# A hybrid convolution and RWKV7 layer on one core: the rows of x transposed by products with a diagonal instead of normalised first

## The chip, the core and the metric

The kernel runs on one core of a Trainium2 chip. The metric is the device time of one execution in microseconds (us), the median over several runs. The engines of the core are TensorE (PE in the profile, its weight loads apart as PEld), VectorE (DVE), ScalarE (ACT), GpSimd (POOL) and SyncE (SP). SP does nothing here but issue DMAs; the queues of DMA issues are called SPq, ACTq and POOLq. Each engine takes its instructions in the order of the program, and an instruction that waits holds up all that stand behind it on its engine.

## The reference

One layer of a decoder over a prompt of 2048 positions and a sample of 8 sequences of 8 positions, D = 1024 columns. Cut to what matters:

```python
xn = rms_norm(x, norm_g)                 # x * rsqrt(mean(x*x) + 1e-6) * norm_g
p = xn @ w_in                            # 1024 -> 4 * 512 + 4 * 512 + 128 columns
# conv branch: u = C * h; causal convolution of width 3; out = B * z * silu(G)
# rwkv7 branch: two-tap token shift of its columns, decay and learning rate by small matrices,
#   S_t = S_{t-1} diag(w_t) + (S_{t-1} (-kk_t)) (kk_t * a_t)^T + v_t k_t^T ;  o_t = S_t r_t
#   per-head group norm, bonus, silu gate
y = concat(y_conv, y_rwkv) @ w_out
y_out = rms_norm(x + y, final_norm_g)
new_shift = xn[:, -1]                    # last normalised row of the prompt and of each sample sequence
```

All inputs and outputs are float32. The change concerns the first line alone, and `new_shift`, which are rows of its result.

## The kernel before, in words

The products with `w_in` contract over D, so they need the normalised rows with D on the partitions: xn transposed. The prompt is worked in two halves of 1024 positions; in each half the columns (positions) are split into three blocks, of 330 (74 for the sample, 256 prompt), 384 and 384 columns in the first half, of 256, 384 and 384 in the second. `xprep(hf)` (lines 211 to 290) prepares a half, block by block:

- Rows come in by SP's queue as tiles of 128 rows x 1024 columns (the sample as 64 x 1024), into staging tiles: four slots "hp", and once each "la" (la1), "wr" and "na", which belong to later stages (line 247).
- ScalarE squares each tile and adds up its rows (line 251); VectorE makes the inverse roots r of up to three tiles at once by three Newton steps on 128x3 (`rsqrt`, line 188).
- Each tile is multiplied by r (one number per row) and by the norm weight, which a DMA has spread over all 128 partitions in a tile "la" (`grow`): one VectorE instruction (line 267), or for the third tile of blocks 1 and 2 a ScalarE copy and a GpSimd product (lines 264 and 265).
- TensorE transposes the tile in pieces of 128x128, four to a PSUM bank "ax" (two buffers; lines 279 and 286).
- `split` (line 205) evacuates a bank: ScalarE rounds it to the high part "xh" (fp32r), VectorE subtracts that from the bank and gets the low part "xl".

`project` (line 309) makes 128 columns of p for each block with 24 matmuls into one PSUM bank "pj" (two buffers): xh by wh, xl by wh, xh by wl, for each of eight k.

The main loop (lines 930 to 972) goes through eight "pairs" of heads, four for each half. A pair projects its columns, forms chunk matrices, inverts triangular chunk matrices (`inverse`, line 640) and runs the recurrence (`wkv`). `inverse` begins with a chain of small VectorE steps on tiles "xi", "sub" and "na" (a forward substitution), whose result goes to DRAM in two DMAs as "dx" (line 669) and comes back re-ordered in twelve DMAs to tiles AB0, AB1, AB2 (line 678); VectorE then transposes each of these in blocks of 32 (line 680) for the next matmuls. `xprep(0)` stands at the start of the program; `xprep(1)` stands in pair 3, behind the last conv group of the first half and ahead of that pair's `inverse`. So the rows of the second half are prepared while the substitution of pair 3 runs on VectorE.

The program is written in that order, but the order of the instructions on each engine is laid out before the kernel runs, by a scheduler that takes the instructions of several generators as their inputs come due. It decides in which row of an engine's list a multiplication, a substitution step and an AB transposition stand.

The line numbers 117, 120, 123 and 129 are those of the helpers `copy`, `stt`, `tt` and `mm`, through which most instructions go; there the tiles tell them apart.

## Time and profile before

| | before |
|---|---|
| median of 3 runs | 1622.39 us (1618.18 to 1624.21) |
| the profiled execution | 1613.0 us, span of its instructions 1610.9 us |
| TensorE matmuls (PE) | 1512.1 us busy, 94% of the span, 11088 instructions |
| weight loads (PEld) | 1265.4 us, 79% |
| VectorE (DVE) | 1011.3 us, 63% |
| ScalarE (ACT) | 616.2 us, 38% |
| GpSimd (POOL) | 289.6 us, 18% |
| mean granted clock of TensorE | 0.969 |

The page of the profile cuts the span into 40 slices of some 40 us and prints the busy share of each engine in tenths:

```profile
PE   4999999999999999989999999999999999899997
DVE  6377458765687458784586358545864578466544
ACT  6443346324542354344541354135313543342221
```

TensorE is at 9 nearly everywhere, but at 4 in the first slice, which holds `xprep(0)`. A slice is too wide for `xprep(1)`, which falls into the eighteenth (685 to 725 us); it shows in windows of 10 us. The percentages are means over stages: what an edit is worth is read in the stage where it stands.

### The profile page before, as it was taken

How to read it: one execution, taken by the hardware profiler on the slowest of the kernel's cores; microseconds unless marked ns; L12 is line 12 of the kernel's file. 1: busy time of each engine (PE TensorE's matmuls, PEld its weight loads, DVE VectorE, ACT ScalarE, POOL GpSimd, SP SyncE). 2: the span in 40 equal slices, each digit the busy share in tenths (PEclk: the TensorE clock that was granted, in tenths of full speed). 3: DMA queues.
4: the chain of work that ended last, by engine and by line, in shares of the span. 5: the costliest groups of instructions: out<-in, count | busy, mean ns of one | idle time of the engine just before them, and what ended most of it. 6: DMA issues, size and time to landing. Idle time of an engine off the chain costs nothing.

```text
span 1610.9 us, 29335 instructions
## 1 busy us (share of the span) xinstructions
PE 1512.1 (94%) x11088; PEld 1265.4 (79%) x11088; DVE 1011.3 (63%) x3101; ACT 616.2 (38%) x1591; POOL 289.6 (18%) x395
## 2 busy tenths in 40 slices
PE   4999999999999999989999999999999999899997
PEld 4989778887788777877789678877897788567885
DVE  6377458765687458784586358545864578466544
ACT  6443346324542354344541354135313543342221
POOL 3134103311133112320022002200220022000000
PEclk9989999899999998999999899999999999899999
DMA  7323412342043213441124112411241145414441
GB/s 241 118 83 110 137 49 74 108 122 78 20 136 113 95 50 112 140 125 61 36 73 125 42 36 66 135 39 37 77 127 38 34 118 155 133 62 137 143 137 53
DMA packets 121967, 151.90 MB, mean 94 GB/s; under 512 B 62617, under 2 KB 86681, under 8 KB 121826
## 3 DMA queue, kind: packets, MB, share of 16 engines
q1 hardware_dynamic: 107024, 104.53, 21.2%
q0 software_dynamic: 9536, 34.64, 6.8%
q10 hardware_dynamic: 5266, 10.86, 1.9%
q8 instruction: 88, 1.44, 0.4%
q14 instruction: 53, 0.43, 0.1%
HBM read 92.60 MB, written 57.35 MB: 93 GB/s over the span
## 4 chain that ended last, share of the span: by engine, by line
PE 63%; DVE 23%; issue 5%; DMA 5%; ACT 2%; POOL 1%; SPq 1%; ACTq 0%; DVEq 0%; POOLq 0%
PE pj L129 41%; PE ca L129 5%; PE ax L129 5%; DVE sub L123 5%; PE cb L129 4%; DVE xi L123 4%; DVE hp L123 2%; PE oo L129 2%; PE cx L129 2%; DVE hp L120 1%; PE cx L703 1%; DVE bk L123 1%; DVE t L120 1%; DMA dx<-xi 1%; DMA AB<-dx 1%
## 5 line engine op out<-in xcount | busy, mean ns | idle before, releaser
L129 PE MATMUL pj<-xh,wh 128*128 128x384 f32 (+3 forms) x1856 | 655.4, 354 | 18.0 <-DVE hp L123 13.8
L129 PE MATMUL pj<-xl,wh 128*128 128x384 f32 (+3 forms) x1856 | 652.8, 352 | 2.7 <-POOL xl L207 2.1
L129 PE MATMUL pj<-xh,wl 128*128 128x384 f32 (+3 forms) x1856 | 650.9, 351 | 0.8 <-DMA wl<-wsp 0.8
L129 PEld LDWEIGHTS pj<-xh,wh 128*128 128x128 f32 x1856 | 356.7, 192 | 50.1 <-DVE hp L123 11.5
L129 PEld LDWEIGHTS pj<-xl,wh 128*128 128x128 f32 x1856 | 356.8, 192 | 31.7 <-POOL xl L207 3.0
L129 PEld LDWEIGHTS pj<-xh,wl 128*128 128x128 f32 x1856 | 355.8, 192 | 27.3 <-issue 1.7
L117 ACT ACTIVATE tS<-sv,wc 64x64 f32<-64x64 f32 x256 | 88.0, 344 | 114.8 <-DVE sv L120 94.2
L207 POOL TENSOR_TENSOR wl<-wr,wh 128x512 fp32r<-128x512 f32 x66 | 87.8, 1342 | 193.4 <-ACT wh L117 190.0
L120 DVE SCALAR_TENSOR_TENSOR sv<-cb,wc,tS 64x64 f32<-64x64 f32 x240 | 68.0, 283 | 62.6 <-PE cb L129 56.1
L129 PE MATMUL ax<-L,bk 64*128 64x128 f32 x528 | 79.1, 298 | 20.9 <-DVE bk L123 11.2
L129 PEld LDWEIGHTS ax<-L,bk 64*128 64x128 f32 x528 | 66.1, 197 | 37.9 <-issue 23.6
L123 DVE TENSOR_TENSOR sub<-xi,na 128x126 f32<-128x126 f32 (+22 forms) x248 | 81.5, 329 | 16.5 <-DMA na<-dn 9.7
L117 ACT ACTIVATE t<-pj,prm 128x384 f32<-128x384 f32 (+3 forms) x170 | 68.8, 433 | 54.5 <-PE pj L129 53.4
L751 DVE TENSOR_SCALAR u<-ca,Q 128x64 f32<-128x64 f32 x128 | 36.2, 283 | 82.3 <-PE ca L129 82.1
L531 POOL TENSOR_TENSOR bk<-t,t 64x384 f32<-64x384 f32 (+2 forms) x56 | 58.3, 1041 | 155.3 <-ACT t L503 72.9
L123 DVE TENSOR_TENSOR xi<-xi,sub 128x126 f32<-128x126 f32 (+22 forms) x248 | 77.6, 313 | 7.1
L117 ACT ACTIVATE wh<-wr 128x512 fp32r<-128x512 f32 x66 | 40.5, 626 | 92.0 <-PE pj L129 73.1
L129 PEld LDWEIGHTS ca<-sv,L 128*64 128x64 f32 x528 | 43.3, 134 | 37.2 <-DVE sv L120 12.8
L129 PE MATMUL ca<-sv,L 128*64 128x64 f32 x528 | 67.8, 245 | 0.1
L741 DVE COPY xs<-ca 128x64 f32<-128x64 f32 x128 | 28.7, 224 | 60.4 <-PE ca L129 50.6
L298 POOL DMA_DIRECT2D wh<-wsp x33 | 18.6, 565 | 254.1 <-PE pj L129 216.7
L123 DVE TENSOR_TENSOR hp<-pj,hp 128x512 f32<-128x512 f32 (+1 forms) x34 | 23.4, 689 | 62.6 <-PE pj L129 62.2
(207 smaller groups left out, 2057.4 us busy)
## 6 DMA issues: line engine op xcount, KB each, us to landing
wr<-in_w_in SPq DMA_DIRECT2D x66, 256.0 KB, 3.7
wsp<-wh SPq DMA_DIRECT2D x33, 512.0 KB, 3.1
wsp<-wl SPq DMA_DIRECT2D x33, 512.0 KB, 3.5
wh<-wsp POOLq DMA_DIRECT2D x33, 512.0 KB, 3.6
wl<-wsp POOLq DMA_DIRECT2D x33, 512.0 KB, 4.8
hp<-in_x_prompt SPq DMA_DIRECT2D x28, 512.0 KB, 4.1
la<-yd SPq DMA_DIRECT2D x16, 512.0 KB, 4.0
out_y_p<-hp ACTq DMA_DIRECT2D x16, 512.0 KB, 2.6
```

The source lines that it names most:

```text
L117: act.activation(out=out, in_=in_, func=AF.Copy, scale=scale, bias=bias)
L120: eng.scalar_tensor_tensor(out=out, in0=in0, scalar=scalar, in1=in1, op0=op0, op1=op1)
L123: dve.tensor_tensor(out=out, in0=in0, in1=in1, op=op)
L129: pe.matmul(out, lhsT=lhsT, rhs=rhs, start=start, stop=stop)
L207: eng.tensor_tensor(out=lo, in0=src, in1=hi.bitcast(F32), op=ALU.subtract)
L298: pool.dma_start(out=wh, in_=wsp[col, 0])
L531: pool.tensor_tensor(out=S.bk[bl.i][hs, chs, h, :], in0=ta[hs, a:a + n].rearrange("p (c j) -> p c j", j=64), in1=wi[hs, a:a + n].rearrange ...
L703: pe.transpose(out=pb[:, i, :], in_=S.bk[bi][:, ca + i].rearrange("p a t -> p (a t)"), identity=ident)
L741: dve.tensor_copy(out=xs_, in_=px)
L751: dve.tensor_scalar(out=u, in0=pu, scalar1=S.Q[:, q:q + 1], scalar2=None, op0=ALU.mult)
```

## The change

The rows are no longer normalised before they are transposed. For each tile of rows VectorE writes a diagonal matrix of the inverse roots (`dg`: the identity, each row times its r; line 260 of the changed kernel), and TensorE multiplies a raw piece of 128x128 by it, which transposes the piece and scales its rows at once. The pieces are ordered by k: one PSUM bank holds one k of all tiles of the block (256 or 384 columns), in turn in "ax", "ax", "cx" (and "oo" in the first half). The norm weight, which is one number per partition once D lies on the partitions, is applied at the evacuation: ScalarE copies the bank times `norm_g` to xh, VectorE forms bank times `norm_g` minus xh in one instruction. For that `norm_g` comes as eight further columns of the parameters; it is no longer spread over partitions for the row tiles. The sample's piece is first multiplied by the weight into a tile "c2" and then split. Since no normalised row exists any more, `shift_rows` computes the nine rows of `new_shift` apart, after the first pair's projections: nine rows loaded, squared, scaled and multiplied by a norm weight spread over nine partitions.

```diff
@@ -37,8 +37,8 @@
-P_MU, P_KK, P_KA, P_RK, P_LG, P_LB, P_W0, P_A0, P_CW = 0, 17, 21, 25, 29, 33, 37, 41, 45
-NPRM = 57
+P_MU, P_KK, P_KA, P_RK, P_LG, P_LB, P_W0, P_A0, P_CW, P_NG = 0, 17, 21, 25, 29, 33, 37, 41, 45, 57
+NPRM = 65
@@ -209,9 +209,6 @@
     WR = T("w", [128, KT, 128], "wr", 1)
 
     def xprep(hf):
-        grow = rowtile()
-        if hf == 1:
-            act.dma_start(out=grow, in_=I["norm_g"].partition_broadcast(128).rearrange("p a d -> p (a d)"))
         if hf == 0:
             act.dma_start(out=cst[:, 0:128], in_=I["consts"][:, 0:128])
         xh, xl = [], []
@@ -252,19 +249,18 @@
                                accum_out=ss[:n, j:j + 1])
                 xts.append(xt)
             if bl.samp:
-                sync.dma_start(out=grow, in_=I["norm_g"].partition_broadcast(128).rearrange("p a d -> p (a d)"))
                 sr = T("small", [128, 144], "sub", 1)[:, :KT * NB].rearrange("p (k b) -> p k b", k=KT)
                 act.dma_start(out=sr, in_=I["state_shift"])
                 load_params()
             dve.tensor_scalar(out=ss, in0=ss, scalar1=1.0 / D, scalar2=RMS_EPS, op0=ALU.mult, op1=ALU.add)
             r = rsqrt(ss, len(rows), 128, "n")
-            for j, xt in enumerate(xts):
-                n = rows[j][1]
-                if bl.i and j == 2:
-                    copy(xt, xt, scale=r[:n, j:j + 1])
-                    pool.tensor_tensor(out=xt, in0=xt, in1=grow[:n], op=ALU.mult)
-                else:
-                    stt(xt, xt, r[:n, j:j + 1], grow[:n])
+            dg = tmp()
+            offs, o = [], 0
+            for j, (_, n, _) in enumerate(rows):
+                dve.tensor_scalar(out=dg[:n, o:o + n], in0=ident[:n, :n], scalar1=r[:n, j:j + 1], scalar2=None,
+                                  op0=ALU.mult)
+                offs.append((o, n))
+                o += n
             if bl.samp:
                 pool.memset(h[:, :, 72:74].bitcast(F32), 0.0)
                 pool.memset(l[:, :, 72:74].bitcast(F32), 0.0)
@@ -272,22 +268,41 @@
                 lv = l[:, :, 0:72].rearrange("p k (b j) -> p k b j", j=9)
                 split(hv[:, :, :, 0], lv[:, :, :, 0], sr)
                 xt = xts.pop(0)
-                rows.pop(0)
-                pool.dma_start(out=O["shift_s"], in_=xt[7:SAMP:8, :])
+                offs.pop(0)
                 ps = AX([128, KT, SAMP])
                 for k in range(KT):
-                    pe.transpose(out=ps[:, k, :], in_=xt[:, k * 128:(k + 1) * 128], identity=ident[:SAMP, :SAMP])
-                split(hv[:, :, :, 1:9], lv[:, :, :, 1:9], ps.rearrange("p k (b j) -> p k b j", j=8))
-            for xt, (_, _, o) in zip(xts, rows):
-                for q in range(2):
-                    ps = AX([128, 4, 128])
-                    for k in range(4):
-                        kk = q * 4 + k
-                        pe.transpose(out=ps[:, k, :], in_=xt[:, kk * 128:(kk + 1) * 128], identity=ident)
-                    split(h[:, q * 4:q * 4 + 4, o:o + 128], l[:, q * 4:q * 4 + 4, o:o + 128], ps)
-            if hf == 1 and bl.i == 2:
-                act.dma_start(out=O["shift_p"], in_=xts[-1][127:128, :])
+                    mm(ps[:, k, :], xt[:, k * 128:(k + 1) * 128], dg[:SAMP, 0:SAMP])
+                sx = T("ch", [128, KT, SAMP], "c2", 4)
+                tt(sx, ps, prm[:, P_NG:P_NG + KT].unsqueeze(2).to_broadcast([128, KT, SAMP]), ALU.mult)
+                split(hv[:, :, :, 1:9], lv[:, :, :, 1:9], sx.rearrange("p k (b j) -> p k b j", j=8))
+            for k in range(KT):
+                tag, nb = (("ax", 2), ("ax", 2), ("cx", 1), ("oo", 1))[k % (4 if hf == 0 else 3)]
+                ps = PS([128, bl.np], tag, nb)
+                for i, (xt, (o, n)) in enumerate(zip(xts, offs)):
+                    mm(ps[:, i * 128:(i + 1) * 128], xt[:, k * 128:(k + 1) * 128], dg[:, o:o + n])
+                hk = h[:, k, bl.c0:bl.c0 + bl.np]
+                copy(hk, ps, scale=pcol(P_NG, k))
+                stt(l[:, k, bl.c0:bl.c0 + bl.np], ps, pcol(P_NG, k), hk.bitcast(F32), ALU.mult, ALU.subtract)
         return xh, xl
+    def shift_rows():
+        n = NB + 1
+        xt = T("pair", [128, 32, 32], "na", 1).rearrange("p a b -> p (a b)")[:n]
+        sync.dma_start(out=xt[0:NB], in_=I["x_sample"][7:SAMP:8, :])
+        sync.dma_start(out=xt[NB:n], in_=I["x_prompt"][SEQ - 1:SEQ, :])
+        junk = T("ch", [128, D], "c2", 4, BF16)[:n]
+        s = T("small", [128, 1], "ss", 2)[:n]
+        act.activation(out=junk, in_=xt, func=AF.Square, accum_out=s)
+        dve.tensor_scalar(out=s, in0=s, scalar1=1.0 / D, scalar2=RMS_EPS, op0=ALU.mult, op1=ALU.add)
+        r = rsqrt(s, 1, n)
+        for q in range(2):
+            m = slice(q * 512, (q + 1) * 512)
+            g = T("ch", [128, 512], "c2", 4)[:n]
+            sync.dma_start(out=g, in_=I["norm_g"].partition_broadcast(n).rearrange("p a d -> p (a d)")[:, m])
+            stt(xt[:, m], xt[:, m], r, g)
+        act.dma_start(out=O["shift_s"], in_=xt[0:NB])
+        act.dma_start(out=O["shift_p"], in_=xt[NB:n])
 
@@ -956,6 +971,8 @@
         if s == 3:
             run(conv_group(xs, hf, p))
             xs = xprep(1)
+        if s == 0:
+            shift_rows()
         run(inverse(S))
         wkv(S)
@@ -989,7 +1006,7 @@
-                                                    "conv_w")], axis=1),
+                                                    "conv_w", "norm_g")], axis=1),
```

Apart from the two stretches of `xprep` and the instructions of `shift_rows`, the lists of before and after hold the same instructions in the same order on each engine. Three places are shown. The numbers in a name tell tiles of one kind apart; a tile keeps its name through its life.

VectorE at the start, from the last step of the first inverse roots ("nwyn" is r; hp_22, hp_23 and hp_24 are the three row tiles of block 0, la0 the spread weight), before:

```order
L120 SCALAR_TENSOR_TENSOR nwyn_26_137<-nwan_27_138,nwyn_26_137 128x3
L120 SCALAR_TENSOR_TENSOR hp_22_121<-hp_22_121,nwyn_26_137,la0_18_115 64x1024
L120 SCALAR_TENSOR_TENSOR hp_23_124<-hp_23_124,nwyn_26_137,la0_18_115 128x1024
L120 SCALAR_TENSOR_TENSOR hp_24_127<-hp_24_127,nwyn_26_137,la0_18_115 128x1024
L207 TENSOR_TENSOR xl0_20_118<-ax_28_158,xh0_19_117 128x8x8x8
L259 TENSOR_SCALAR ssx_35_199<-ssx_35_199 128x3
L194 TENSOR_SCALAR nwan_40_211<-ssx_35_199 128x3
```

And after ("t" is the diagonal, "c2" the sample's weighted piece, cst holds the identity, prm the weight):

```order
L120 SCALAR_TENSOR_TENSOR nwyn_25_135<-nwan_26_136,nwyn_25_135 128x3
L260 TENSOR_SCALAR t_27_148<-cst_1_90,nwyn_25_135 64x64
L260 TENSOR_SCALAR t_27_148<-cst_1_90,nwyn_25_135 128x128 x2
L123 TENSOR_TENSOR c2_29_165<-ax_28_156,prm_4_95 128x512
L255 TENSOR_SCALAR ssx_40_211<-ssx_40_211 128x3
L194 TENSOR_SCALAR nwan_45_223<-ssx_40_211 128x3
L196 TENSOR_SCALAR nwyn_44_222<-nwan_45_223 128x3
L123 TENSOR_TENSOR nwan_45_223<-nwyn_44_222 128x3
L120 SCALAR_TENSOR_TENSOR nwan_45_223<-nwan_45_223,ssx_40_211 128x3
L120 SCALAR_TENSOR_TENSOR nwyn_44_222<-nwan_45_223,nwyn_44_222 128x3
L207 TENSOR_TENSOR xl0_19_117<-c2_29_165,xh0_18_116 128x8x8x8
L120 SCALAR_TENSOR_TENSOR xl0_19_117<-ax_30_169,prm_4_95,xh0_18_116 128x256
```

The three multiplications of whole tiles are gone, two kinds of diagonals stand in their place, and the roots of block 1 (ssx, nwan, nwyn) have moved up ahead of the sample's low part.

VectorE in the middle, where the second half is prepared; xl0, xl1 and xl2 are the low parts of its three blocks, and "na" out of AB0 is the block transposition in `inverse`. Before:

```order
L120 SCALAR_TENSOR_TENSOR hp_1224_7518<-hp_1224_7518,nwyn_1230_7531,la0_1191_7384 128x1024
L120 SCALAR_TENSOR_TENSOR hp_1226_7522<-hp_1226_7522,nwyn_1230_7531,la0_1191_7384 128x1024
L680 STREAM_TRANSPOSE na_1283_7725<-AB0_1065_6328 128x128
L207 TENSOR_TENSOR xl2_1222_7516<-ax_1232_7548,xh2_1221_7515 128x4x128
L207 TENSOR_TENSOR xl2_1222_7516<-ax_1233_7555,xh2_1221_7515 128x4x128
L680 STREAM_TRANSPOSE na_1283_7725<-AB1_1066_6329 128x192
L207 TENSOR_TENSOR xl2_1222_7516<-ax_1234_7562,xh2_1221_7515 128x4x128
L207 TENSOR_TENSOR xl2_1222_7516<-ax_1235_7569,xh2_1221_7515 128x4x128
```

And after:

```order
L120 SCALAR_TENSOR_TENSOR xl0_1210_7437<-ax_1219_7464,prm_4_95,xh0_1209_7436 128x256
L120 SCALAR_TENSOR_TENSOR xl0_1210_7437<-ax_1220_7469,prm_4_95,xh0_1209_7436 128x256
L120 SCALAR_TENSOR_TENSOR xl0_1210_7437<-cx_1221_7474,prm_4_95,xh0_1209_7436 128x256
L260 TENSOR_SCALAR t_1237_7532<-cst_1_90,nwyn_1235_7519 128x128
L120 SCALAR_TENSOR_TENSOR xl0_1210_7437<-ax_1222_7479,prm_4_95,xh0_1209_7436 128x256
L695 STREAM_TRANSPOSE na_1311_7799<-AB0_1083_6380 128x128
L120 SCALAR_TENSOR_TENSOR xl0_1210_7437<-ax_1223_7484,prm_4_95,xh0_1209_7436 128x256
L120 SCALAR_TENSOR_TENSOR xl0_1210_7437<-cx_1224_7489,prm_4_95,xh0_1209_7436 128x256
L120 SCALAR_TENSOR_TENSOR xl0_1210_7437<-ax_1225_7494,prm_4_95,xh0_1209_7436 128x256
L120 SCALAR_TENSOR_TENSOR xl0_1210_7437<-ax_1226_7499,prm_4_95,xh0_1209_7436 128x256
L695 STREAM_TRANSPOSE na_1311_7799<-AB1_1084_6381 128x192
L120 SCALAR_TENSOR_TENSOR xl1_1228_7505<-ax_1238_7536,prm_4_95,xh1_1227_7504 128x384
```

Before, the first transposition of AB0 stood behind the last multiplications of block 2; now it stands between the fourth and the fifth low part of block 0, and that of AB1 ahead of the first low part of block 1.

SP's queue in the middle; "dx" is the way out of the substitution, AB0 to AB2 the way back, "hp" from in_x_prompt the row loads, here those of block 2. Before:

```order
L247 DMA hp_1224_7518<-in_x_prompt 128x1024
L384 DMA yd02_86<-hp_1159_6982 128x384
L247 DMA hp_1226_7522<-in_x_prompt 128x1024
L247 DMA hp_1228_7526<-in_x_prompt 128x1024
L669 DMA dx_1282_7722<-xi_1239_7592 1024x1x32 x2
L678 DMA AB0_1065_6328<-dx_1282_7722 32x4x32 x4
L678 DMA AB1_1066_6329<-dx_1282_7722 32x6x32 x4
L678 DMA AB2_1067_6330<-dx_1282_7722 32x6x32 x4
```

And after:

```order
L684 DMA dx_1310_7796<-xi_1267_7666 1024x1x32 x2
L693 DMA AB0_1083_6380<-dx_1310_7796 32x4x32 x3
L399 DMA yd02_86<-hp_1177_7034 128x384
L693 DMA AB0_1083_6380<-dx_1310_7796 32x4x32
L693 DMA AB1_1084_6381<-dx_1310_7796 32x6x32 x3
L244 DMA hp_1249_7587<-in_x_prompt 128x1024
L244 DMA hp_1251_7591<-in_x_prompt 128x1024
L244 DMA hp_1253_7595<-in_x_prompt 128x1024
L693 DMA AB1_1084_6381<-dx_1310_7796 32x6x32
L693 DMA AB2_1085_6382<-dx_1310_7796 32x6x32 x4
```

The three row loads of block 2, which stood ahead of the dx transfers, now stand ahead of the fourth transfer of AB1.

## Rows read from the trace of the kernel before

**Rows 1.** Busy us by stretch (instruction counts in brackets), clock, DMA, columns in the first line

```profile
core 0: us, PE busy (x) PEld busy (x) DVE busy (x) ACT busy (x) POOL busy (x), PEclk, DMA share, GB/s
690.00:700.00 10.00, 5.58 (x34) 5.31 (x35) 9.31 (x31) 1.86 (x5) 2.42 (x5) 0.94 0.79 260
700.00:710.00 10.00, 10.00 (x64) 9.41 (x64) 5.71 (x14) 6.87 (x13) 0.78 (x3) 0.72 0.66 189
740.00:760.00 20.00, 20.00 (x185) 14.45 (x183) 9.62 (x35) 7.70 (x23) 1.05 (x2) 1.00 0.20 66
```

**Rows 2.** Chain of waits from the start: start us, us, engine, tile, line, instructions

```profile
44.38 38.96 PE pj L129 x233
```

**Rows 3.** Instructions on tile pj alone by stretch; columns PE, PEld, DVE, ACT, clock, DMA

```profile
0.00:44.38 44.38, 13.32 (x56) 10.70 (x57) 0.66 (x2) 1.31 (x4) 1.00 0.65 219
694.90:722.20 27.30, 15.77 (x81) 12.38 (x79) 1.50 (x3) 2.45 (x7) 0.87 0.48 136
```

**Rows 4.** Timeline, start: start us, us, engine line op out<-in, count [idle before <-releaser]

```profile
9.26 0.17 DVE L259 TENSOR_SCALAR ssx<-ssx 128x3 f32<-128x3 f32 x1 [0.31 <-ACT xl L251]
...
11.63 3.90 DVE L120 SCALAR_TENSOR_TENSOR hp<-hp,nwyn,la 64x1024 f32<-64x1024 f32 x3
...
12.96 1.11 PE L279 MATMUL ax<-cst,hp 64*128 64x64 f32 x8 [12.96 <-DVE hp L120]
...
16.19 2.11 PE L286 MATMUL ax<-cst,hp 128*128 128x128 f32 x8 [0.68 <-DVE xl L207]
```

**Rows 5.** Timeline of the middle, where the second half's rows are prepared

```profile
686.83 2.39 POOL L265 TENSOR_TENSOR wr<-wr,la 128x1024 f32<-128x1024 f32 x1 [14.64 <-ACT wr L117]
686.84 3.46 DVE L120 SCALAR_TENSOR_TENSOR hp<-hp,nwyn,la 128x1024 f32<-128x1024 f32 x1
...
690.82 0.45 PE L129 MATMUL pj<-xh,wh 128*128 128x384 f32 x1 [1.45 <-DVE t L120]
...
695.09 1.04 PE L286 MATMUL ax<-cst,hp 128*128 128x128 f32 x8
...
699.73 2.18 PE L286 MATMUL ax<-cst,hp 128*128 128x128 f32 x8 [3.60 <-DVE xl L207]
...
703.01 1.29 SPq L669 DMA_DIRECT2D dx<-xi  x2
...
708.92 6.66 SPq L678 DMA_DIRECT2D AB<-dx  x12
```

**Rows 6.** Nearest operations: timeline rows, and groups by form (busy us, mean ns | idle before)

```profile
651.14 0.90 PE L129 MATMUL ax<-L,bk 64*128 64x128 f32 x6 [0.87 <-DVE bk L123]
...
712.28 0.47 DVE L120 SCALAR_TENSOR_TENSOR t<-pj,omm,t 128x256 f32<-128x256 f32 x1
...
736.55 0.62 DVE L120 SCALAR_TENSOR_TENSOR t<-pj,omm,t 128x384 f32<-128x384 f32 x1 [0.86 <-ACT t L117]
...
L129 PE MATMUL ax<-L,bk 64*128 64x128 f32 x528 | 79.1, 298 | 20.9 <-DVE bk L123 11.2 <-DVE nwag L120 4.3 <-DVE L L123 3.0
...
L207 DVE TENSOR_TENSOR xl<-ax,xh 128x512 fp32r<-128x512 f32 x33 | 22.2, 687 | 9.0 <-ACT xh L117 8.9
...
L117 ACT ACTIVATE xh<-ax 128x512 fp32r<-128x512 f32 x33 | 19.2, 595 | 17.5 <-PE ax L286 14.9 <-POOL sv L775 2.1
...
L251 ACT ACTIVATE xl<-hp 128x1024 fp32r<-128x1024 f32 x6 | 6.3, 1054 | 3.3 <-DMA hp<-in_x_prompt 3.1
```

**Rows 7.** Timeline of pair 0, from the dx issues to the first AB transposition

```profile
167.32 1.30 SPq L669 DMA_DIRECT2D dx<-xi  x2
...
171.71 3.68 SPq L678 DMA_DIRECT2D AB<-dx  x8
...
174.52 0.30 DVE L680 STREAM_TRANSPOSE na<-AB 128x128 f32<-128x128 f32 x1
```

**Rows 8.** DMAs landed in 700 to 720 us: KB each, median us from issue to landing

```profile
hp<-in_x_prompt SPq DMA_DIRECT2D x2, 512.0 KB, 4.2
AB<-dx SPq DMA_DIRECT2D x8, 24.0 KB, 1.9
```

## The prediction

> **What bounds the kernel now.** I read the engines' busy time by stretch first, then the chain of waits for the start, then the timeline of the two stretches in which the rows of x are prepared. TensorE is the bound: it is busy for the whole of a normal stretch, 20.00 of 20 us at 740 [rows 1], and from 44.38 us on the chain runs for 38.96 us through 233 projection matmuls without a break, 0.167 us each [rows 2]. The rows are prepared twice, and only there is TensorE short of work: before 44.38 us, and from 690 to 722 us, where it sits idle and its granted clock falls to a mean of 0.72 from 700 to 710 [rows 1]. So the change is worth what it does to the moment at which the projections run unbroken, in each of the two places. What it saves on VectorE elsewhere costs nobody anything.
>
> In those two places the work of TensorE before "unbroken" is known: 56 projection matmuls had started by 44.38, and 81 by 722.2, three of them of the conv group before [rows 3]. I count against these.
>
> The profiled execution took 1613.0 us with a span of 1610.9; the median of the runs is 1622.39. I work in the profiled execution and add the difference to the median.
>
> **The change part by part.** *Removed:* 17 multiplications of a whole row tile. The 13 on VectorE cost 1.3 us each (three in 3.90) [rows 4], but 3.46 when GpSimd multiplied at the same time, as at 686.84 [rows 5]; the other four were a ScalarE copy and a GpSimd product. Also removed: 32 pairs of 512-wide evacuations, 0.59 us on ScalarE and 0.69 on VectorE [rows 6], and in each half one load of the norm weight, spread over 128 partitions (128 x 1024 x 4 bytes, 512 KB).
>
> *Added on TensorE:* each of the 128 transpositions of 128x128 becomes a float32 product. Eight transpositions at full clock take 1.04 us [rows 5], about 0.11 from one to the next when the tail of the last (some 0.3) is taken off. A float32 product appears as two records: the three products of a head in the attention matrices (line 547) are six records, 0.90 us at 651.14, and one lasts 0.30 in the mean [rows 6], so 0.12 from one to the next for 128 columns. A product is thus 0.22 us or a little more, at half clock 0.43; transpositions at half clock, eight in 2.11 with one pause, bear the doubling out [rows 4]. That is +0.11 x 64 = 7 us of TensorE in each place. It lies on the path where TensorE is what is waited for, else beside a wait.
>
> The Trainium skill ("TensorE: Matmul & The Clock Gate", section "Terms") says that the transpose mode is four times as fast for FP32. By it a product would cost 0.44 against 0.11 and each place would gain 21 us of TensorE, not 7. The two records of 0.11 to 0.12 in this trace make it twice, and I use those.
>
> *Added on ScalarE and VectorE:* 48 pairs of evacuations, 256 or 384 wide. Nearest rows with PSUM as source: ScalarE 0.59 for 512 columns, VectorE 0.47 and 0.62 for 256 and 384 [rows 6]; back to back some 0.08 less. A block of 384 costs some 8 x 0.5 = 4 us on ScalarE and 8 x 0.55 = 4.4 on VectorE, where it was 6 x 0.6 and 6 x 0.69 and two multiplications. The diagonal is a 128x128 TENSOR_SCALAR that no row shows: between 0.17 (three columns) and 0.47 (256 from PSUM) [rows 4, 6]; I take 0.25, nearer to the small one since its source is SBUF, so 0.75 a block.
>
> *The start.* The square roots end at 11.63 as before: the load of the norm weight stood behind the first rows in the queue. The first diagonal replaces the first multiplication, so TensorE starts near 12.0 where it started at 12.96 [rows 4]. Sample rows: 8 x 0.22 = 1.7 us at half clock (half the columns). Block 0: 16 products, 6.9 us at half clock, so 20.6; at full clock from the middle on, 18. ScalarE is as late: its order now puts weight rounding and a square (1.05 [rows 6], and its read) between the copies. Last low part of block 0: 21.5. Diagonals of block 1: 22.2. Block 1 goes at ScalarE's pace: 8 x 0.5 and two squares, 6.5 us from the first copy, so low parts end at 30. Nine of the twelve root steps of block 2 follow (all of them 2.4 us, from 9.26 to 11.63 [rows 4]), then its diagonals: 32.6. Block 2: 24 products 5.2 us, 5.1 on ScalarE: 38. By then the order has 45 projections behind it instead of 56; the 11 missing cost 1.9. The time comparable to 44.4 is 39.9: a gain of 4.5 us. Bounds: 2 if ScalarE and TensorE alternate badly over the four banks, 7 if block 1 starts as soon as its rows have landed. The separate norm of the nine shift rows, some 20 small instructions on VectorE and one square, falls into 44 to 84 us, where VectorE is idle; it would cost its 4 us only without that cover.
>
> *The middle.* VectorE ends the substitution of the inverse (xi, sub) before the row preparation; the dx issue at 703.01 marks its end [rows 5]. It loses four multiplications, 3 x 1.3 + 3.46 = 7.4 us, and three 0.69 evacuations that stood among its steps, so it ends near 693.5. The conv group's last projection no longer waits 1.45 us at 690.82 for VectorE [rows 5]; block 0 starts about 694 instead of 695.09. So far a gain. Two waits then come to stand at the head of VectorE's queue.
>
> First, the transposition of AB (line 680, now 695) stands between the fourth and the fifth low part of block 0; before, it came behind the last multiplications. AB comes back through DRAM. From the dx issue to the AB issue: 4.4 us in pair 0, 5.9 in this place [rows 5, 7]. Twelve issues take 6.66, 0.55 each; four and a yd store in between: 2.6; landing 1.9 [rows 8]. So AB is there at 702.5 to 704, and VectorE stands before it from 698. Behind it wait four low parts of block 0. With three PSUM banks in turn (ax, ax, cx) TensorE gets three products further and stops: about 5 us idle.
>
> Second, the last three row loads now stand in SP's queue ahead of the fourth AB copy of block 1. They need the slot of a row tile of block 0, whose last product waited above. A load lands after 4.2 us [rows 8]; ScalarE's square of it stands between the third and the fourth copy of block 1, and VectorE's second transposition waits for the AB copy behind 1.5 MB. If that copy takes its usual 1.9 us, this wait is 1 us, else up to 4; ScalarE stands until 707 to 708 either way. I take 4 us idle on TensorE.
>
> The Trainium skill ("DMA: Bandwidth & Descriptors", section "Queues, rings and completion order") says that SP has one ring on each DMA engine, consumed in ring order. By it the copy comes behind all of the 1.5 MB, the 4 us; by the row of AB alone, 1 us. The trace leans to the rule: dx behind two row loads took 5.9 instead of 4.4.
>
> Block 1 then takes until 714, the squares, roots (2.4) and diagonals of block 2 until 717.5, its products with three banks 5.5: 723. The order has 53 projections of the second half done there; before, 78 at 722.1. The difference is 0.9 + 25 x 0.167 = 5.1 us; with one more microsecond for the granted clock, which fell here before in the idle stretch, 6 us lost. Bounds: 12 lost if both waits are at their long end and the clock is half through block 2; 4 gained if neither ends later than the evacuations. Behind 722 TensorE is full again, so the loss is not made up.
>
> Sum: -4.5 + 6 = +1.5 us, 1614.5 in the profiled execution, 1624 on the median.
>
> **The rivals.**
>
> *A: no new wait decides.* The AB copies and row loads come in time. For it: VectorE sheds 7.4 us just there, and the chain from dx to the transposition in pair 0 was 7.2 us in all [rows 7]. Against: from 693.5 even that ends at 701. Then block 2 would end near 713.5, with 53 projections behind it; the 25 missing bring it to 718, 4 us before 722. With the start at 5: -9, 1613.
>
> *B: the two waits grow and TensorE slows down.* One mechanism: the head of VectorE's queue waits for AB, TensorE idles about 5 and 5 us, its clock goes to half as it did in this place [rows 1], and block 2's 24 products at 0.43 take 10.3. Middle +12, start -2: +10, 1632. It decides from some 9 us of idle time on.
>
> *C: only the start counts.* The waits are as long as the time that VectorE won; the middle is even. -4.5, 1618. For it: the wait of 3.60 us at 699.73 for VectorE disappears [rows 5].
>
> *D: products at double price*, as at half clock, in both places: 64 x 0.22 more on the path, of which the middle bears some 13: +12, 1634. Against: the row at 651.14. The skill's factor of four would be of this kind, and worse.
>
> **How the numbers follow.** Forecast 0.50, A 0.13, B 0.18, C 0.15, D 0.04. About 0.5% (8 us) is what a measurement of this kernel can tell from no change. Faster by more than that: A and 0.02 of C, 0.15. Slower: B, D and 0.01 of the forecast's tail, 0.23. Within: the rest, 0.62. The range goes from A to B with the runs' own spread: 1612 to 1634. The likeliest case alone: 1618 to 1629.
>
> **What would show it.** Right: projections unbroken from about 39 us; the transposition on line 695 waiting several microseconds for AB, low parts of xl right behind it; TensorE idle twice between 697 and 710 of the old time scale; two records per product, 0.11 apart at full clock. Wrong: flow in the start not before 42; the substitution still ending last; block 2 finished before the old 718; or a loss elsewhere, in the pairs that the change does not touch.

## The result, and the profile after

The changed kernel took 1633.48 us (median of 19 runs, 1619.58 to 1640.38), the kernel before 1622.62 (19 runs, 1607.45 to 1629.79): ratio 1.0065, interval 1.0043 to 1.0087. So it is slower by 10.9 us, where the forecast said 1.5.

Runs of one kernel lie up to 25 us apart, and each run but those first 19 of before lists its span and mean granted clock. Over these runs of all kernels, each kernel about its own mean, the span falls by 1.34 us for each 0.001 of clock. With that slope I put the spans to a clock of 0.967; what is left of a kernel's spread is a standard deviation of some 2 us. The kernel before then has 1618.7 ± 0.2 us (80 runs, mean clock 0.9672), the changed one 1628.1 ± 0.3 (31 runs, 0.9658): 9.4 us more work or waiting. The other 1.9 us lie in a clock lower by 0.0014 ± 0.0009, which these runs don't tell from chance. The runs come from several chips, and these errors leave the chip out: the kernel before has 1617.8 ± 0.3, 1618.9 ± 0.4, 1619.7 ± 0.6 and 1621.0 ± 0.4 us on four of them. So a difference between kernels is safest against before on the same chip; there after_again, the changed kernel run again, is 10.1 ± 0.5 us slower. The profiled execution of the changed kernel took 1622.11 us, span 1620.3, mean clock 0.972. It lies 11 us under its median, as that of before lies 10 under its own, so the two traces can be laid side by side.

Its page gives TensorE 1524.8 us busy instead of 1512.1, VectorE 1000.4 instead of 1011.3, and this line of TensorE by slices:

```profile
PE   6989999989999999989999899999999999899997
```

The first slice rises from 4 to 6, yet the moment from which the projections run unbroken tells a smaller gain. The chain of waits of the changed kernel, the row of the start (start us, us, engine, tile, line, instructions):

```profile
42.26 40.40 PE pj L129 x240
```

The instructions on tile pj by stretch (us, then busy and count for PE, PEld, VectorE, ScalarE, then clock, DMA share, GB/s), at the start and in the middle:

```profile
0.00:42.26 42.26, 9.06 (x49) 7.43 (x49) 0.75 (x2) 1.39 (x4) 1.00 0.63 212
...
694.90:724.10 29.20, 9.73 (x56) 7.20 (x54) 1.03 (x2) 1.84 (x5) 0.94 0.52 148
```

At the start the unbroken stretch begins 2.12 us earlier than in [rows 2], but with 49 projections behind it instead of 56 [rows 3]: 2.12 - 7 x 0.167 = 1.0 us gained, where 4.5 were forecast. In the middle the last product runs about 724.1, with 56 projections behind it where 81 had been made by 722.2 [rows 3]: 1.9 + 25 x 0.167 = 6.1 us lost, where 6 were forecast.

The start in the timeline of the changed kernel (columns as in [rows 4]):

```profile
11.40 0.64 DVE L260 TENSOR_SCALAR t<-cst,nwyn 64x64 f32<-64x64 f32 x3
11.70 5.68 PE L129 MATMUL ax<-t,hp 64*128 64x64 f32 x24 [11.70 <-DVE t L260]
...
22.74 1.26 POOL L207 TENSOR_TENSOR wl<-wr,wh 128x512 fp32r<-128x512 f32 x1 [1.73 <-ACT wh L117]
23.11 1.38 DVE L260 TENSOR_SCALAR t<-cst,nwyn 128x128 f32<-128x128 f32 x3
24.19 0.46 PE L129 MATMUL ax<-t,hp 128*128 128x128 f32 x2 [1.03 <-issue]
...
31.25 0.61 DVE L120 SCALAR_TENSOR_TENSOR xl<-oo,prm,xh 128x384 fp32r<-128x384 f32 x1
31.68 1.29 POOL L207 TENSOR_TENSOR wl<-wr,wh 128x512 fp32r<-128x512 f32 x1 [7.68 <-ACT wh L117]
31.77 1.22 DVE L123 TENSOR_TENSOR nwan<-nwyn 128x3 f32<-128x3 f32 x1
33.02 0.39 DVE L120 SCALAR_TENSOR_TENSOR nwan<-nwan,ssx 128x3 f32<-128x3 f32 x1
33.45 0.48 DVE L120 SCALAR_TENSOR_TENSOR nwyn<-nwan,nwyn 128x3 f32<-128x3 f32 x1
33.96 0.16 DVE L123 TENSOR_TENSOR nwan<-nwyn 128x3 f32<-128x3 f32 x1
...
35.52 1.58 PE L129 MATMUL ax<-t,hp 128*128 128x128 f32 x12 [1.17 <-issue]
36.94 0.83 PE L129 MATMUL cx<-t,hp 128*128 128x128 f32 x6
37.61 0.83 PE L129 MATMUL oo<-t,hp 128*128 128x128 f32 x6
```

TensorE starts at 11.70 (forecast 12.0). Six records take 37.61 - 36.94 = 0.67 us: 0.112 a record, 0.223 a product, as forecast. But three diagonals beside GpSimd's weight rounding take 1.38 instead of 0.68 (at 35.13); the first root step shown of block 2 takes 1.22 beside the next rounding, and the two behind it 0.39 and 0.48 beside two casts of GpSimd (from 32.92 to 33.92), where the next takes 0.16.

The middle (columns as before; SPq is SP's queue):

```profile
693.71 1.30 SPq L684 DMA_DIRECT2D dx<-xi  x2
695.13 1.05 PE L129 MATMUL ax<-t,hp 128*128 128x128 f32 x8
697.58 0.71 PE L129 MATMUL ax<-t,hp 128*128 128x128 f32 x4 [0.83 <-DVE xl L120]
699.50 1.34 SPq L693 DMA_DIRECT2D AB<-dx  x3
703.22 0.31 DVE L695 STREAM_TRANSPOSE na<-AB 128x128 f32<-128x128 f32 x1 [3.90 <-DMA AB<-dx]
703.42 2.39 SPq L244 DMA_DIRECT2D hp<-in_x_prompt  x3
703.96 1.15 PE L129 MATMUL ax<-t,hp 128*128 128x128 f32 x4 [3.63 <-DVE xl L120]
706.05 0.37 DVE L695 STREAM_TRANSPOSE na<-AB 128x192 f32<-128x192 f32 x1
709.06 1.05 ACT L248 ACTIVATE c<-hp 128x1024 bf16<-128x1024 f32 x1
717.24 0.68 DVE L260 TENSOR_SCALAR t<-cst,nwyn 128x128 f32<-128x128 f32 x3
717.63 1.58 PE L129 MATMUL ax<-t,hp 128*128 128x128 f32 x12 [0.58 <-PE pj L129]
```

The first forecast wait is there: the AB transposition stands 3.90 us in VectorE's queue, and TensorE idles 3.63. The second is not: the transposition of AB1 and the squares of block 2 wait for nothing. The three waits of TensorE in this excerpt (0.83, 3.63, 0.58) are all it has from 690 to 724, 5.04 us; before they were 1.45 at 690.82 and 3.60 [rows 5], and two small ones (0.66 and 0.39), 6.10 in all. So TensorE waits no longer here than before, and loses time all the same.

I therefore added up every TensorE record from 600 to 860 us: the usual distance from one start to the next for its kind is work, what half clock (1.2 GHz) adds is clock, the rest is waiting. (The waits are more than the idle time, since a matmul counts as busy up to its modelled end, and other stages lie in the stretch. A stretch is bounded by the same two projections in each trace.)

| 600 to 860 us of the program | whole | work | half clock | waits |
|---|---|---|---|---|
| before (first trace) | 260.0 | 178.8 | 7.3 | 73.9 |
| before (second trace) | 258.9 | 178.6 | 6.3 | 74.0 |
| changed (first trace) | 260.1 | 186.6 | 2.5 | 70.8 |
| changed (second trace) | 263.0 | 186.7 | 5.3 | 70.9 |
| products back to transpositions | 262.3 | 178.5 | 5.5 | 78.3 |

The work rises by 8 us, as 64 x (0.223 - 0.107) = 7.4 says; waits fall by 3. Without the clock that is 4.9 us lost. Behind the preparation, too, up to some 850 us, the two traces differ in more than these tiles: TensorE's matmuls of the recurrence stand elsewhere among the projections. So the section on the change is wrong in saying that the lists agree outside the two stretches and `shift_rows`, and the 4.9 us hold this difference as well.

### The profile page after: what moved, and what is told of

Read it like the earlier page. It is cut to its first block, busy times and chain, and to the rows that moved or that the text cites. A ratio compares the mean times of both kernels' runs of the same rounds, so it can differ in the third digit from the quotient of the medians.

```text
span 1620.3 us, 29660 instructions
## 1 busy us (share of the span) xinstructions
PE 1524.8 (94%) x11224; PEld 1278.4 (79%) x11224; DVE 1000.4 (62%) x3136; ACT 617.7 (38%) x1605; POOL 277.4 (17%) x390
## 4 chain that ended last, share of the span: by engine, by line
PE 64%; DVE 21%; DMA 5%; issue 4%; ACT 2%; SPq 1%; POOL 1%; ACTq 0%; DVEq 0%; POOLq 0%
PE pj L129 41%; PE ax L129 6%; PE ca L129 5%; DVE sub L123 5%; DVE xi L123 4%; PE cb L129 4%; PE oo L129 2%; PE cx L129 2%; DVE hp L123 2%; DMA dx<-xi 1%; PE cx L718 1%; DVE bk L123 1%; DVE t L120 1%; DMA AB<-dx 1%; DVE t L510 1%
## 5 line engine op out<-in xcount | busy, mean ns | idle before, releaser
L117 ACT ACTIVATE tS<-sv,wc 64x64 f32<-64x64 f32 x256 | 87.9, 344 | 115.5 <-DVE sv L120 94.9
L123 DVE TENSOR_TENSOR sub<-xi,na 128x126 f32<-128x126 f32 (+22 forms) x248 | 78.7, 317 | 17.0 <-DMA na<-dn 10.1
```

What stands on the lines that cost most here:

```text
L117: act.activation(out=out, in_=in_, func=AF.Copy, scale=scale, bias=bias)
L123: dve.tensor_tensor(out=out, in0=in0, in1=in1, op=op)
```

## The experiments

Beside each ratio (with its interval, against the kernel before run on the same chip) stands the span at clock 0.967, as above, with its standard error, and last how far that lies above before on the same chip (after_again and the three that follow it ran on one chip, the others on three more).

| kernel | median us, runs | ratio | clock | span at 0.967 | above before on its chip |
|---|---|---|---|---|---|
| before | 1622.62, 19 | 1 | 0.9672 | 1618.7 ± 0.2 | 0 |
| after_again | 1631.62, 12 | 1.0062 (1.0027 to 1.0098) | 0.9667 | 1627.9 ± 0.4 | 10.1 ± 0.5 |
| shift_rows_only | 1620.64, 12 | 1.0001 (0.9967 to 1.0036) | 0.9672 | 1619.5 ± 0.4 | 1.7 ± 0.5 |
| first_half_only | 1621.34, 12 | 1.0006 (0.997 to 1.0043) | 0.9677 | 1620.0 ± 0.3 | 2.2 ± 0.5 |
| second_half_only | 1628.78, 12 | 1.005 (1.0014 to 1.0087) | 0.9659 | 1626.5 ± 0.6 | 8.7 ± 0.6 |
| ab_late | 1627.91, 12 | 1.0058 (1.0026 to 1.0089) | 0.9683 | 1628.2 ± 0.6 | 9.3 ± 0.8 |
| raw_second | 1636.36, 12 | 1.0125 (1.0086 to 1.0163) | 0.9602 | 1626.2 ± 0.9 | 7.3 ± 1.0 |
| row_scale_second | 1648.45, 6 | 1.0166 (1.0118 to 1.0215) | 0.9587 | 1634.6 ± 1.2 | 15.7 ± 1.3 |
| raw_first | 1628.93, 12 | 1.0042 (1.0018 to 1.0065) | 0.9647 | 1623.7 ± 0.5 | 4.0 ± 0.7 |
| shift_late | 1636.16, 6 | 1.0092 (1.0061 to 1.0123) | 0.9638 | 1629.5 ± 0.4 | 9.8 ± 0.7 |
| raw_second_ab_late | 1633.8, 6 | 1.0085 (1.0056 to 1.0113) | 0.9615 | 1626.3 ± 0.8 | 6.6 ± 1.0 |
| squares_late_ab_late | 1634.71, 5 | 1.0094 (1.0077 to 1.0111) | 0.9644 | 1628.7 ± 0.9 | 7.8 ± 1.0 |

### Which part carries the loss

My theory: the loss is in the second half, from the waits behind AB. The rivals: the start, the shift rows, or the price of the products wherever they stand. Four kernels take the change apart. Unchanged runs:

> The changed kernel as it stands, to have a second trace of it and the granted clock of every run of both kernels. Theory A (the loss lies in the two places where rows are prepared): again 8 to 13 us above before at the median, and the steps of +1 to +3 us that the first trace shows in later pairs (at 105, 145, 310, 450, 820, 900 and 1060 us) fall elsewhere or are missing this time. Theory B (the change moves GpSimd's work against VectorE's, and the loss is made in the pairs): the steps at 105 and 145 us stand in the same place with the same size, and so do most of the others.

> The kernel before as it stands, for a second trace of it. All five other traces show 1 to 3 us more TensorE idle time than the first trace of before in each of the stretches 100 to 200, 280 to 400 and 400 to 600 us, where the order of the instructions is the same. If that is chance, this trace shows it too; if the changed start causes it, it does not.

The kernel before with `shift_rows` alone. Both halves use `xprep_rows`, which is before's `xprep` without the two stores of `new_shift`; first_half_only has only the second of these edits on the changed kernel, second_half_only only the first:

```diff
-    xs = xprep(0)
+    xs = xprep_rows(0)
-            xs = xprep(1)
+            xs = xprep_rows(1)
```

> The kernel before with the nine output rows computed apart (shift_rows) and nothing else of the change. Theory A: within 1.5 us of before, since its instructions fall where VectorE is idle. Rival C (the nine rows hold the tile na, which the substitution of pair 0 needs, and their DMAs and VectorE steps collide with pair 0): 3 to 8 us above before, with the loss between 100 and 165 us.

> The changed kernel with the rows of the second half prepared in the old way (normalised, then transposed). Theory A: 1 to 5 us below before, as my sum has it for the start (-4.5), or about -0.7 by the first trace of the changed kernel. Theory B (loss made in the pairs after a changed start): 5 to 12 us above before.

> The kernel before with the change in the second half alone (and the nine rows apart). Theory A: 4 to 12 us above before (my sum: 6), VectorE standing some 4 us before AB at its transposition and TensorE idle right behind it. Theory B: within 2 us of before, although that wait is there.

before_again took 1620.22 us in its one run (span 1618.3, clock 0.968). Against before on the same chip, the shift rows cost 1.7 ± 0.5, the first half another 0.5, the second half another 7.0; together 9.2 of the 10.1. So the second half carries most of the loss, and the first half brings nothing: the 1 to 5 us below before that I had expected of first_half_only did not come, while second_half_only lies in its 4 to 12 above. In shift_rows_only and first_half_only the scheduler also laid out parts behind 760 us in another order; second_half_only keeps the changed kernel's order from the middle on. That touches the 7.0: reckoned as in the table of 600 to 860 us, the traces of second_half_only and shift_rows_only differ by 3.8 us in that stretch and by another 3.4 from 1200 to 1590 us, where only the order differs.

### The wait for AB, and the price of a product

If the loss is the wait, moving the transposition behind block 0 takes it away. A copy of one element makes the transposition depend on block 0's last low part; the order of nearly all else stays (a few projections, squares and evacuations and the transposition of AB1 move by some places; `late` is set in pair 3 alone):

```diff
+            if late[0] and bl.i == 0:
+                dve.tensor_copy(out=t1[0:1, 0, 0:1], in_=xs[1][0][0:1, KT - 1, 255:256].bitcast(F32))
```

> The changed kernel with the transposition of AB0 in pair 3 tied behind the last low part of block 0 (a one-element copy makes it wait for that), so that no low part of block 0 stands behind the DMA of AB. Theory V (the wait of 3.9 us at 703 costs TensorE 3.6 us and about as much again later): 4 to 8 us below the changed kernel. Theory W (the wait has only taken the place of an older one of 3.6 us, the loss is TensorE work): 2 to 4 us below, the idle gap of 3.63 us and no more.

In raw_second the second half's pieces are transposed with the plain identity, at the price of before; the inverse roots are left out, and with them the wait for the diagonals:

```diff
+                    if hf == 0:
                         mm(ps[:, i * 128:(i + 1) * 128], xt[:, k * 128:(k + 1) * 128], dg[:, o:o + n])
+                    else:
+                        pe.transpose(out=ps[:, i * 128:(i + 1) * 128], in_=xt[:, k * 128:(k + 1) * 128], identity=ident)
```

> The changed kernel, but the 64 products of the second half are plain transpositions of the raw rows by the identity; the inverse root is left out of that half's result (the diagonals are still computed). Theory W (TensorE's doubled price per piece is on the path: 64 x 0.11 = 7 us more work where TensorE is the bound): 5 to 9 us below the changed kernel, that is -3 to +5 us against before. Theory V (VectorE's wait for AB is what the second half costs): within 2 us of the changed kernel, since that wait stays.

ab_late gained nothing that the runs can tell: 1628.2 against 1628.1, and by the same chip 9.3 ± 0.8 against 10.1 ± 0.5. By its own terms both theories fail, V with 4 to 8 us and W with 2 to 4; of W's "idle gap and no more" the gap went, and the time stayed. TensorE's waits there, with the AB transposition and the first square of block 2 (the middle lies some 6 us later in this trace):

```profile
703.57 0.71 PE L129 MATMUL ax<-t,hp 128*128 128x128 f32 x4 [0.83 <-DVE xl L120]
708.80 0.31 DVE L699 STREAM_TRANSPOSE na<-AB 128x128 f32<-128x128 f32 x1 [0.94 <-DMA AB<-dx]
709.66 0.49 PE L129 MATMUL cx<-t,la 128*128 128x128 f32 x2 [0.66 <-DVE xl L120]
712.18 0.49 PE L129 MATMUL ax<-t,la 128*128 128x128 f32 x2 [0.91 <-DVE xl L120]
713.63 1.06 ACT L248 ACTIVATE c<-hp 128x1024 bf16<-128x1024 f32 x1 [2.42 <-DMA hp<-in_x_prompt]
715.96 0.49 PE L129 MATMUL ax<-t,la 128*128 128x128 f32 x2 [1.28 <-DVE xl L120]
722.36 1.63 PE L129 MATMUL ax<-t,hp 128*128 128x128 f32 x12 [1.38 <-issue]
```

The 3.63 us are gone, and 0.66 + 0.91 + 1.28 + 1.38 stand in their place: 5.06 us with the first, where it was 5.04. Now ScalarE's square waits 2.42 us for its rows: the second wait that I had forecast appears once the first has gone. That the wait for AB had hidden it is the likeliest reading; no trace shows it by itself.

raw_second takes 1.9 ± 0.9 us off at equal clock (2.8 ± 1.1 by the same chip), not 7.4; W had said 5 to 9, V at most 2. Its work falls to before's 178.5 us, and its waits rise from 70.8 to 78.3 (table above). The largest wait in the timeline of its TensorE:

```profile
709.99 0.47 PE L285 MATMUL cx<-cst,la 128*128 128x128 f32 x1 [2.41 <-DVE xl L120]
```

And its clock is 0.9602, 0.0056 ± 0.0017 under that of the changed kernel, worth 7.5 us (ab_late, on the same chip, had 0.9683); so on the median it is slower than the kernel whose work it lightens.

row_scale_second keeps the roots, with transpositions: raw pieces, the roots spread over the partitions by a product of ones with the diagonal, and one more VectorE multiplication for each bank:

```diff
+                    mm(ps[:, i * 128:(i + 1) * 128], ones, dg[:, o:o + n])
+                copy(rr[:, :bl.np], ps)
...
+                    u = tmp()[:, :bl.np]
+                    stt(u, ps, pcol(P_NG, k), rr[:, :bl.np])
+                    split(hk, l[:, k, bl.c0:bl.c0 + bl.np], u)
```

> Second half: rows transposed raw with the identity, then multiplied on VectorE by the norm weight and by a row of the inverse roots that one product with a matrix of ones per row tile has spread over the partitions; then split as before. TensorE work per row tile: 8 x 0.107 + 0.22 instead of 8 x 0.223. Theory W: 3 to 6 us below the changed kernel, less than raw_second, if VectorE's second instruction per bank (some 0.5 us x 24) is hidden; Theory V: no better than the changed kernel.

It is the slowest of all: TensorE's waits from 600 to 860 us rise to 87.6 us, the longest of them for VectorE (3.13 us), a weight load (2.70) and ScalarE (2.53), and its clock is the lowest. VectorE's second instruction for each bank is not hidden.

### The start, the shift rows, and two waits at once

The remaining questions: what holds the start, whether the place of `shift_rows` costs anything, and whether work and waits together give the middle back. raw_first is raw_second's edit with `hf == 1` for `hf == 0`; it leaves out the first half's roots. shift_late:

```diff
-        if s == 0:
+        if s == 7:
             shift_rows()
```

> The changed kernel, but the 64 prompt products of the first half are plain transpositions of the raw rows by the identity; the inverse root is left out of that half's result (the diagonals are still computed). If TensorE's doubled price is what used up the forecast gain of the start: 3 to 6 us below the changed kernel. If the start is paced by ScalarE's evacuations and VectorE's roots and diagonals: within 1.5 us.

> The changed kernel with the nine output rows (shift_rows) computed in the last pair instead of the first; the start, the middle and all between have the same order as in the changed kernel. In every trace with shift_rows in pair 0, 100 to 200 us takes 2 to 3 us longer than in the two traces of before. If shift_rows is the cause: 1.5 to 3 us below the changed kernel at equal granted clock, and the stretch back at 100 us. Rival (the changed start has moved GpSimd's weight rounding against VectorE's steps in pair 0): no gain, and the stretch as long as in the changed kernel.

raw_second_ab_late has the edits of both, and leaves out the second half's roots:

> Second half with both edits: plain transpositions by the identity (the inverse root left out of that half's result) and AB0's transposition tied behind the last low part of block 0. Each alone moved the time at equal clock by -2 (transpositions) and 0 us (AB). If TensorE's work and the waits behind AB and behind the row loads bind in turn, each covering the other: 3 to 7 us below the changed kernel at equal clock, more than the two together. If something else sets the end of the stretch (the order of the projections behind it): again about -2.

squares_late_ab_late has ab_late's edit and one that sets the three squares of block 2 behind block 1's last copy:

```diff
+                if hf == 1 and bl.i == 2 and j == 0:
+                    copy(ss[0:1, 0:1], xh[1][0:1, KT - 1, 383:384].bitcast(F32))
```

> The changed kernel with both forecast waits taken out of the way in the second half: AB0's transposition stands behind the last low part of block 0, and ScalarE's three squares of the rows of block 2 stand behind the last copy of block 1 (each by a one-element copy that they must wait for). With the first edit alone the second wait appeared instead (ScalarE waited 2.42 us for the row loads, TensorE 0.91, 1.28 and 1.38 us) and nothing was gained. Theory V (the waits cost TensorE their length): 2 to 4 us below the changed kernel at equal granted clock, TensorE's waits between 700 and 725 us down from 5 to under 2.5. Theory W (the work of 64 products is the loss and the waits only exchange places): within 1 us, a wait of block 2 for its roots and diagonals in their place.

raw_first takes 4.4 ± 0.6 us off (6.1 ± 0.9 by the same chip), about the 3 to 6 expected if the doubled price ate the gain. The chain of waits shows where:

```profile
37.76 40.53 PE pj L129 x240
```

It runs unbroken from 37.76 instead of 42.26 us. The distance of its transpositions, in the timeline of its TensorE:

```profile
25.38 0.27 PE L285 MATMUL ax<-cst,hp 128*128 128x128 f32 x1
25.49 0.27 PE L285 MATMUL ax<-cst,la 128*128 128x128 f32 x1
25.59 0.27 PE L285 MATMUL ax<-cst,na 128*128 128x128 f32 x1
```

0.105 us each, against 0.223 for a product. So at the start the doubled price and the two waits for diagonals (1.03 and 1.17 us) eat the gain. The edit takes both away, and the scheduler then lays the pieces out among the projections, so it doesn't tell the shares apart. The Trainium skill ("Perfetto Trace Analysis", section "Transposes") advises to use a transposition rather than a standard matmul for what is logically one; the start agrees by these 4.4 us, the middle, where waits fill up, by 1.9 ± 0.9 only.

shift_late gains nothing (1629.5; 9.8 by the same chip), so the place of `shift_rows` costs no time. raw_second_ab_late gains no more than raw_second alone (1626.3 and 1626.2). In its trace TensorE's waits from 699 to 725 us add up to 8.4 us, and the longest is for the row loads of block 2 themselves:

```profile
711.79 0.45 PE L285 MATMUL cx<-cst,hp 128*128 128x128 f32 x1 [4.53 <-DMA hp<-in_x_prompt]
```

In squares_late_ab_late TensorE's waits change place once more:

```profile
701.82 0.71 PE L129 MATMUL ax<-t,hp 128*128 128x128 f32 x4 [0.83 <-DVE xl L120]
709.01 0.49 PE L129 MATMUL cx<-t,la 128*128 128x128 f32 x2 [1.76 <-DVE xl L120]
720.46 1.58 PE L129 MATMUL ax<-t,hp 128*128 128x128 f32 x12 [2.67 <-issue]
```

5.26 us again, now most of it at block 2's diagonals, and the span is 1628.7. By the same chip it is 2.3 ± 1.1 us under the changed kernel, so these five runs don't settle whether it gains V's 2 to 4 us or, as W has it, nothing; the waits, which V wanted under 2.5 us, stayed. No version here beats the kernel before.

## Why the prediction was right or wrong

**The sum.** Forecast +1.5 us, measured +10.9. That 1633.48 still lies inside the stated 1612 to 1634, by half a microsecond, is luck: the upper end was set for rival B and the runs' own spread, and B's mechanism didn't happen. The likeliest case alone (1618 to 1629) missed.

**The middle: right in sign, in size partly by luck.** Forecast +6, one of it for the clock. Measured +7.0 ± 0.7 at equal clock by second_half_only against shift_rows_only, of which 3.4 may be the other order behind 1200 us; 6.1 by the count in the profile, 4.9 without the clock from 600 to 860 us, the order behind the preparation included. The end of the substitution (693.5; the issue of dx shows 693.71), AB's return (702.5 to 704; 703.22), the diagonals of block 2 (717.5; 717.24) and the end (723; 724.1) came as forecast. But of the 9 us of idling that carried the size only 3.63 came, and the clock worked the other way: half clock took 7.3 and 6.3 us in the stretch before, 2.5 and 5.3 after.

**Its words name the wrong cause.** The text said that two waits come to stand at the head of VectorE's queue. The first only took the place of the 3.60 us at 699.73 [rows 5]; TensorE's waits there add up to 5.0 to 5.3 us in every variant that keeps the products, whichever wait I removed. What rose is TensorE's own work, the 7.4 us of doubled products, which the step on added work sized rightly and then put partly "beside a wait". Yet the price alone isn't the cause either: with it gone, waits took its place, 7.5 us of them in raw_second. Beside TensorE's products runs a second chain, through AB, the slots of row tiles, row loads, squares, roots and diagonals. The changed order by k lengthens it: a row tile comes free only at its block's last product, and the row loads of block 2 stand behind the AB issues and are issued at 703.42, where before they stood ahead of dx. That this chain is what takes the place is argued from such rows, the 4.53 us for row loads in raw_second_ab_late above all. The runs say this much: easing either chain alone, or the price and AB together, gives back 2 us at most by the pooled spans, and up to 3.5 ± 1.1 by the same chip. A kernel with the price gone and both waits moved was not run, and the raw kernels also drop the wait for diagonals and change the order of some neighbours from 700 to 900 us; so how the 7 us divide stays open.

**The second wait was misread.** I forecast 4 us idle because the fourth copy of AB1 is issued behind the row loads. The transposition of AB1 at 706.05 waits for nothing: it needs only the columns that the first copies fill, not the ones of the copy behind the row loads. ab_late shows a shorter wait in its place, 2.42 us on ScalarE for the rows themselves. The ring rule that I weighed ("DMA: Bandwidth & Descriptors" in the Trainium skill) is therefore not tested here. What I took for a sign of it falls: from dx to AB it took 5.79 us again (693.71 to 699.50), with no row load just ahead of dx.

**The start: wrong.** Forecast -4.5, measured +0.5 ± 0.5 by first_half_only against shift_rows_only, and a gain of 1.0 by the count in the profile. The step that failed is the pace from block 1 on. Until the end of block 0's products (20.6; 20.5) the times came as forecast, the last although the products were 0.11 us a record from 18 on (0.21 before that), where the text had reckoned with half clock; it had ScalarE as late. The diagonals were priced at 0.75 a block; those of block 1 took 1.38, and the first product of block 1 came at 24.19 instead of some 22. Low parts of block 1 ended at 31.86, not 30; the nine root steps and diagonals behind them, 2.6 us in the forecast, took until the first product at 35.52, 3.7 us. Block 2 ended near 40.9, not 38. The bound of "2 if ScalarE and TensorE alternate badly" was still too kind: I had counted these small VectorE steps at their undisturbed length, and nothing for GpSimd beside them. raw_first shows the other term, the doubled price with its waits for diagonals, which is on the path here.

**About 2 us were not forecast at all.** They lie from 100 to 200 us, in pair 0. Without the clock, that stretch takes 94.9 and 95.0 us in the two traces of before and more in every other: 97.2 and 96.6 in the changed kernel, 97.5 in shift_late, and 98.4 and 98.5 in shift_rows_only and second_half_only, whose start is the old one. So neither the changed start nor the place of `shift_rows` makes it. Two instructions of VectorE and GpSimd there swap their speeds, and TensorE waits for a later product of VectorE; before, and then after:

```profile
103.88 3.46 POOL L531 TENSOR_TENSOR bk<-t,t 64x384 f32<-64x384 f32 x2 [1.47 <-DVE t L120]
104.19 0.54 DVE L123 TENSOR_TENSOR L<-hp,W 128x384 f32<-128x384 f32 x1
106.63 0.90 PE L129 MATMUL ax<-L,bk 64*128 64x128 f32 x6 [1.07 <-DVE bk L123]
107.90 1.33 PE L129 MATMUL ax<-L,bk 64*128 64x128 f32 x6 [0.37 <-DVE bk L123]
```

```profile
103.26 2.53 POOL L546 TENSOR_TENSOR bk<-t,t 64x384 f32<-64x384 f32 x2 [1.48 <-DVE t L120]
103.56 1.38 DVE L123 TENSOR_TENSOR L<-hp,W 128x384 f32<-128x384 f32 x1
108.46 1.57 PE L129 MATMUL ax<-L,bk 64*128 64x128 f32 x12 [3.53 <-DVE bk L123]
```

The first two start 0.31 and 0.30 us apart, and once the one is slow, once the other; TensorE waits 3.53 us instead of 1.44. shift_rows_only shows the slow form as well:

```profile
103.16 1.37 DVE L123 TENSOR_TENSOR L<-hp,W 128x384 f32<-128x384 f32 x1
108.05 2.28 PE L129 MATMUL ax<-L,bk 64*128 64x128 f32 x12 [3.52 <-DVE bk L123]
```

So the two microseconds can account for the 1.7 of shift_rows_only, and not for the first half's +0.5, which is measured against it. What makes the swap stays open: the kernels that show it share the separate rows and the eight further columns of parameters.

**The rest.** The place of `shift_rows` costs nothing, but the kernel that has it alone is 1.7 ± 0.5 us above before (0.8 by the pooled spans), where none was forecast. The price of a product was right (0.22; 0.223); rival D fell. Rival B named the right median (1632) by a mechanism that didn't happen: there was no second 5 us of idling, and the clock from 700 to 710 us rose from 0.72 to 0.83. The windows of the changed kernel (columns as in [rows 1]):

```profile
700.00:710.00 10.00, 6.37 (x40) 6.07 (x40) 3.99 (x9) 3.41 (x6) 0.35 (x3) 0.83 0.74 227
740.00:760.00 20.00, 19.98 (x169) 14.17 (x165) 9.58 (x26) 7.92 (x22) 2.15 (x4) 1.00 0.31 101
```

At 740 TensorE is full again, as said, so nothing is made up. On the chip of the first experiments, at equal clock, the changed kernel lies 10.1 above before. Between the forecast's +1.5 and that lie 5.0 us of the first half, 1.0 of the second, 1.7 of the shift rows (pair 0 among them) and 0.9 that the parts apart don't show.

## What to carry to other kernels

Moving arithmetic from an engine that waits (VectorE) into instructions of the engine that bounds the kernel adds to the work of that engine (8 us here, where the waits fell by 3); count its work and its waits apart before and after. Here a wait that was taken away uncovered the next one of nearly the same length: add up the waits of the bounding engine in the stretch, and ask for the length of the second chain before pricing the first. Small instructions on a shared path are to be priced at what they take beside their neighbour, not alone. And a control kernel is itself laid out anew by the scheduler: see where its trace differs before its time is subtracted.

## What the runs showed of the hardware

- The granted clock makes most of the spread of one kernel: 1.34 us of span for 0.001 of mean clock. At equal clock twelve runs give a mean to 0.3 to 0.9 us, but chips differ: before took 1617.8 us at clock 0.967 on one and 1621.0 on another.
- At the start TensorE's records come at half pace, though the clock column prints 1.00 there: projections of 330 columns were 0.275 us apart at 28 us in the kernel before, and 0.155 at 21 us in the changed one, whose TensorE had been busy for all 8 us from 12 to 20 (4.52 us before).
- Less work for TensorE can go with less clock: raw_second and row_scale_second, in which it waits more, were granted 0.960 and 0.959 against 0.966.
- VectorE steps of 128x3 take 0.16 us alone, 1.22 beside a GpSimd product and 0.39 and 0.48 beside its casts; three diagonals 0.68 and 1.38. The Trainium skill ("GPSIMD Engine Reference", section "1. Specifications") says that GpSimd shares its SBUF interfaces with VectorE; these rows, and the two of pair 0, agree. Which of the two is slowed can change from kernel to kernel at the same distance, as the last pair shows.
